# A two-layer hybrid block on one core: squares of the delta rule's rows taken four heads at a time

## The chip, the cores and the metric

The kernel runs on one core of a Trainium2 chip. The metric is device time in microseconds of one execution. The kernel before took 1170.36 us (median of three runs, 1169.89 to 1171.27).

Engines are named as in the profile: PE multiplies matrices and transposes through the identity (PEld loads its weights), DVE and ACT are the vector and the scalar engine, POOL the general one, SP issues DMAs. Each engine works through its own queue in the order in which the program was built, and an instruction at the head of a queue that waits for a semaphore holds up everything behind it.

## What is computed

256 positions of width 1024 go through two layers of `ffn`, `mixer`, `ffn`, `ple` and a last RMS norm. The mixer adds an attention over key blocks (NSA) and a gated delta rule with 4 heads of 128. Of the delta rule this matters:

```
gq, gk, gv = silu(conv(qkv)) split in three
gq, gk = x * rsqrt(sum(x * x) + 1e-6) per head
o = gated_delta_rule(gq, gk, gv, log_decay, beta)     # q is scaled by 128 ** -0.5
o = rmsnorm(o, gdn_norm) * silu(zg)
out = concatenate([o_nsa, o]) @ w_out
```

## The kernel before

Rows of x stand in two tiles of 128 positions. Every dense product is taken as three products of 128x128 by 128x512, of a high and a low part of both factors (`mm3`). Weights come by DMA in units of 128x2048, each cut into two halves; ACT writes the high part (`hi`, L158) and DVE the low part (`lo`, L159). There are five buffers each for `hi` and `lo`, so ACT can only write a high part when PE has done the last product with the one five before it.

A mixer runs seven generators side by side (`weave`, L452): the dense products of w_in (`dense`), the delta rule (`keys`, `queries`, `values`), the gates, the attention, and the output product (`project`). A `yield` hands over to another one. `weave` follows PE's planned time alone, so the order of emission has no costs of ACT, DVE or POOL in it. The framework then schedules the emitted instructions again, engine by engine, by costs of its own and by the readiness of operands and buffers; the queues that result are what runs.

The steps that the change touches, per layer:

- `squares` (L737) gives the sums of squares of the four heads of k (from `gdn_keys`, L753) and of q (from `gdn_queries`, L877), for both tiles of 128 positions. Source is a PSUM bank of 128x4x128: four ACT instructions with an accumulator each, and a `junk` output.
- From q's sums POOL makes `rqs` (L878 to L880): the norm of q, with the scale 128 ** -0.5.
- `gdn_outputs` (L925) computes the delta rule's rows `o` without q's norm; ACT copies them out of PSUM (L935).
- `gdn_finish` (L938) squares `o * rqs` per head (L947, ACT), POOL takes the power (L948, L949), DVE multiplies the two norms (L950) and then rows, norm and gate (L953); PE transposes the result (L957), ACT and DVE split it in `g` (L961, L962), on which the second half of the output product waits.

The output product (`pairs`, L342, called at L552) has 96 wide products per layer: 48 on the attention's result (`n`), then 48 on the delta rule's (`g`). They are the last work of PE in a mixer.

The attention's softmax takes, for the second tile of positions, four score banks per pair of heads: DVE adds the mask and takes the maximum (L1063), ACT does the exponential (L1070) and the scaling (L1079), PE transposes, ACT copies (L1091, `pT`), PE multiplies by the values. The output gate `zg` is the last of the dense chunks: ACT copies it (L486) and does its tanh (L695), DVE finishes it (L696). Two buffers under the tag `m2` serve the tanh, the gated rows and, in the changed kernel, the squares.

Of the kernel before, what the change touches and what calls it, by code (L numbers as in the profile page):

```python
# [12 lines left out]
BF = mybir.dt.bfloat16  # L13
AF = mybir.ActivationFunctionType
OP = mybir.AluOpType
AX = mybir.AxisListType
# [9 lines left out]
EPS = 1e-6  # L26
# [143 lines left out]
class Kern:  # L170
# [565 lines left out]

    def squares(self, ss, src):  # L737

        for h in range(4):
            junk = self.tile("junk", [128, 128], BF)  # L740
            self.nc.scalar.activation(junk, src[:, h], AF.Square, accum_out=ss[:, h:h + 1])

    def gdn_keys(self, g):

# [180 lines left out]
    def gdn_outputs(self, g):  # L925

        nc = self.nc
        g["o"] = o = self.tile("g", [128, NT, 4, 128], name="o")
        for t in range(NT):
            b = self.bank("G", [128, 4, 128])  # L930
            for h in range(4):
                if t:
                    self.mm(b[:, h], g["qe"][:, h], g["st"][:, h], True, False)
                self.mm(b[:, h], g["attn"][:, t, h], g["vn"][t][:, h], not t, True)
            nc.scalar.activation(o[:, t], b, AF.Copy)  # L935
            yield 0.4

    def gdn_finish(self, g, szg):  # L938
        nc, l, os = self.nc, self.l, g["o"]
        oh, ol, get = self.parts("g", 4)  # L940
        for t in range(NT):
            o = os[:, t]
            ss, f = self.tiny(4, "oss"), self.tiny(4, "of")
            rqs = g["rqs"][:, t]
            for h in range(4):
                junk = self.tile("junk", [128, 128], BF)
                nc.scalar.activation(junk, o[:, h], AF.Square, scale=rqs[:, h:h + 1], accum_out=ss[:, h:h + 1])  # L947
            nc.gpsimd.tensor_scalar(f, ss, 1.0 / 128, EPS, op0=OP.mult, op1=OP.add)  # L948
            nc.gpsimd.tensor_tensor(f, f, self.mhalf[:, :4], op=OP.pow)  # L949
            nc.vector.scalar_tensor_tensor(f, f, 0.5, rqs, op0=OP.mult, op1=OP.mult)  # L950
            og = self.tile("m2", [128, 4, 128])
            for h in range(4):
                nc.vector.scalar_tensor_tensor(og[:, h], o[:, h], f[:, h:h + 1], szg[:, t, h * 128:(h + 1) * 128],  # L953
                                               op0=OP.mult, op1=OP.mult)
            b = self.bank("G", [128, 4, 128])
            for h in range(4):
                self.tr(b[:, h], og[:, h])  # L957
            yield 0.5
            gn = self.sm[:, l, S_GN:S_GN + 1]
            ts = slice(t * 128, (t + 1) * 128)  # L960
            nc.scalar.activation(oh[0][:, :, ts], b, AF.Copy, scale=gn)  # L961
            nc.vector.scalar_tensor_tensor(ol[0][:, :, ts], b, gn, oh[0][:, :, ts].bitcast(F32),  # L962
                                           op0=OP.mult, op1=OP.subtract)
        g["gdn"] = get
# [177 lines left out]
```

## Time and profile before

| what | us |
|---|---|
| median of three runs | 1170.36 |
| the profiled execution | 1169.91 |
| its span, first to last instruction | 1168.1 |
| PE busy | 1143.6 |
| DVE busy | 727.9 |
| ACT busy | 666.1 |
| POOL busy | 66.5 |

The execution's own time is 1.8 us above its span. Of the span, the first mixer takes about 202 to 367 us and the second about 778 to 942 us, read from the chain of waits; the rest are feed-forward parts and `ple`. "Busy" of PE is modelled to a product's end, so that overlapping products count once and a sparse PE can still read as nearly busy.

### The profile page before, as it was taken

The page shows a single profiled execution, that of the slowest core. Times are in us where ns is not written, and L with a number is a line of the kernel's source. Part 1 is how long each engine was busy: PE and PEld are TensorE (multiplying, and loading weights), DVE is VectorE, ACT ScalarE, POOL GpSimd, SP SyncE. Part 2 cuts the span into 40 slices and gives each one's busy share as a digit, 9 for nine tenths or more (in the row PEclk, how much of TensorE's full clock was granted, in tenths as well). Part 3 has the DMA queues.
Part 4 walks back from the last instruction along what each step waited for, and adds up shares of the span by engine and source line. Part 5 has one row for each costly group of instructions (what it writes and reads, how often), then busy time and mean ns, then how long its engine had stood idle before and what let it go on. Part 6 is the DMA issues. An engine that isn't in the chain of part 4 may idle for free.

```text
span 1168.1 us, 16007 instructions
## 1 busy us (share of the span) xinstructions
PE 1143.6 (98%) x6182; PEld 924.5 (79%) x6182; DVE 727.9 (62%) x1233; ACT 666.1 (57%) x1217; POOL 66.5 (6%) x94
## 2 busy tenths in 40 slices
PE   8999999999999999999999999999999999999996
PEld 6888888878767888888878888887787678888885
DVE  5656545897756565645675555469978466555454
ACT  7545445746886454544665454366479665545363
POOL 0000000030020000000000000002300100000011
PEclk9999999999999999999999999999999999999998
DMA  8545754531114545554454565544322245455640
GB/s 325 186 176 202 259 187 137 198 139 74 70 47 147 208 172 188 188 212 150 180 204 157 216 226 207 193 155 162 109 73 100 75 151 206 156 215 190 202 176 36
DMA packets 29291, 194.27 MB, mean 166 GB/s; under 512 B 3232, under 2 KB 3616, under 8 KB 7200
## 3 DMA queue, kind: packets, MB, share of 16 engines
q1 hardware_dynamic: 28496, 191.69, 45.2%
q10 hardware_dynamic: 720, 1.57, 0.4%
q8 instruction: 48, 0.79, 0.3%
q14 instruction: 27, 0.22, 0.1%
HBM read 192.20 MB, written 1.05 MB: 165 GB/s over the span
## 4 chain that ended last, share of the span: by engine, by line
PE 90%; DVE 5%; ACT 3%; issue 1%; POOL 1%; DMA 0%; POOLq 0%; SPq 0%; ACTq 0%
PE bA L267 51%; PE bN L267 31%; PE bG L271 4%; PE bG L267 3%; DVE lo L159 1%; PE bN L271 1%; ACT hi L158 1%; ACT p L1079 1%; DVE mn L628 0%; DVE mn L618 0%; DMA x<-x 0%; DVE mn L622 0%; ACT junk L947 0%; POOL rqs L879 0%; DVE ad L786 0%
## 5 line engine op out<-in xcount | busy, mean ns | idle before, releaser
L267 PE MATMUL bA<-hi,xT 128*128 128x512 f32 (+1 forms) x1856 | 600.6, 396 | 0.9 <-DVE xT L321 0.5
L159 DVE TENSOR_TENSOR lo<-raw,hi 128x1024 fp32r<-128x1024 f32 (+2 forms) x358 | 430.6, 1207 | 214.8 <-ACT hi L158 193.7
L158 ACT ACTIVATE hi<-raw 128x1024 fp32r<-128x1024 f32 (+2 forms) x358 | 373.1, 1047 | 225.6 <-PE bN L267 122.7
L267 PEld LDWEIGHTS bA<-hi,xT 128*128 128x128 f32 x1856 | 344.2, 188 | 70.0 <-ACT xT L320 1.9
L267 PE MATMUL bA<-lo,xT 128*128 128x512 f32 (+1 forms) x928 | 360.5, 390 | 0.0
L267 PEld LDWEIGHTS bA<-lo,xT 128*128 128x128 f32 x928 | 174.9, 188 | 34.3 <-issue 1.2
L267 PE MATMUL bN<-hi,n 128*128 128x512 f32 x448 | 144.9, 396 | 1.9 <-ACT n L1101 1.9
L267 PE MATMUL bN<-hi,g 128*128 128x512 f32 x448 | 139.9, 391 | 0.0
L267 PEld LDWEIGHTS bN<-hi,n 128*128 128x128 f32 x448 | 84.3, 189 | 21.2 <-ACT n L1101 2.8
L267 PEld LDWEIGHTS bN<-hi,g 128*128 128x128 f32 x448 | 83.8, 188 | 17.2
L383 DVE SCALAR_TENSOR_TENSOR m<-bA,r,m 128x256 f32<-128x256 f32 x88 | 42.2, 479 | 79.5 <-ACT m L381 79.5
L267 PE MATMUL bN<-lo,n 128*128 128x512 f32 x224 | 89.6, 400 | 0.0
L267 PE MATMUL bN<-lo,g 128*128 128x512 f32 x224 | 87.8, 392 | 0.0
L381 ACT ACTIVATE m<-bA,r 128x256 f32<-128x256 f32 x88 | 41.4, 470 | 72.7 <-PE bA L267 69.6
L292 POOL TENSOR_SCALAR r<-ss 128x1 f32<-128x1 f32 x18 | 6.0, 331 | 839.4 <-ACT junk L285 839.4
L267 PEld LDWEIGHTS bN<-lo,n 128*128 128x128 f32 x224 | 42.6, 190 | 8.0 <-issue 0.2
L267 PEld LDWEIGHTS bN<-lo,g 128*128 128x128 f32 x224 | 42.1, 188 | 8.4
L321 DVE SCALAR_TENSOR_TENSOR xT<-bG,first,xT 128x128 fp32r<-128x128 f32 x96 | 31.6, 346 | 24.8 <-ACT xT L320 24.7
L389 ACT ACTIVATE g<-bG 128x256 fp32r<-128x256 f32 x48 | 18.0, 374 | 42.4 <-PE bG L271 42.3
L320 ACT ACTIVATE xT<-bG,first 128x128 fp32r<-128x128 f32 x96 | 32.7, 361 | 16.0 <-DVE xT L321 15.8
L271 PE MATMUL bG<-first,m 128*128 128x128 f32 x192 | 38.4, 277 | 2.0 <-DVE m L953 1.8
L271 PEld LDWEIGHTS bG<-first,m 128*128 128x128 f32 x192 | 26.3, 141 | 16.7 <-DVE m L953 3.1
(229 smaller groups left out, 957.4 us busy)
## 6 DMA issues: line engine op xcount, KB each, us to landing
raw<-up SPq DMA_DIRECT2D x86, 1024.0 KB, 4.8
raw<-dn SPq DMA_DIRECT2D x44, 1024.0 KB, 4.8
raw<-win SPq DMA_DIRECT2D x24, 1024.0 KB, 4.8
raw<-wout SPq DMA_DIRECT2D x8, 1024.0 KB, 4.9
raw<-gate SPq DMA_DIRECT2D x8, 1024.0 KB, 4.7
cw<-cw SPq DMA_DIRECT2D x8, 512.0 KB, 7.7
raw<-up SPq DMA_DIRECT2D x4, 512.0 KB, 6.7
raw<-proj SPq DMA_DIRECT2D x2, 1024.0 KB, 4.8
```

Of the source, the lines that this page charges most:

```text
L158: nc.scalar.activation(hi[:, s:f], raw[:, a + s:a + f], AF.Copy)
L159: nc.vector.tensor_tensor(lo[:, s:f], raw[:, a + s:a + f], hi[:, s:f].bitcast(F32), op=OP.subtract)
L267: self.nc.tensor.matmul(out, lhsT, rhs, start=start, stop=stop, skip_group_check=part)
L271: self.nc.tensor.transpose(out, x, self.ident[:n, :n])
L292: nc.gpsimd.tensor_scalar(r, self.ss[:, 0:1], self.ss[:, 1:2], EPS, op0=OP.add, op1=OP.add)
L320: nc.scalar.activation(hi[h][:, i, cs], b[:, i, :], AF.Copy, scale=g)
L321: nc.vector.scalar_tensor_tensor(lo[h][:, i, cs], b[:, i, :], g, hi[h][:, i, cs].bitcast(F32), op0=OP.mult, op1=OP.subtract)
L381: nc.scalar.activation(s, bs[t][:, :256], AF.Silu, scale=r[t])
L383: nc.vector.scalar_tensor_tensor(h, bs[t][:, 256:], r[t], s, op0=OP.mult, op1=OP.mult)
L389: nc.scalar.activation(hh[c // 2][o], b, AF.Copy)
L1079: nc.scalar.activation(p[kv][:, i, br], p[kv][:, i, br], AF.Copy, scale=m[:, i, br:br + 1])
```

## The change

k's and q's squares become one ACT instruction over 128x512 into an `m2` tile in 32 bits, and one DVE sum over the last axis. The rows `o` leave PSUM on DVE, times `rqs`, in place of ACT's copy. Their squares go the same new way, `rqs` is no longer a scale of the square, and the factor 0.5 and the second multiplication by `rqs` (L950) go into the constants of L948: f = (4 sum / 128 + 4 eps) ** -0.5.

```diff
     def squares(self, ss, src):
-        for h in range(4):
-            junk = self.tile("junk", [128, 128], BF)
-            self.nc.scalar.activation(junk, src[:, h], AF.Square, accum_out=ss[:, h:h + 1])
+        sq = self.tile("m2", [128, 4, 128])
+        self.nc.scalar.activation(sq, src, AF.Square)
+        self.nc.vector.tensor_reduce(ss, sq, axis=AX.X, op=OP.add)
...
-            nc.scalar.activation(o[:, t], b, AF.Copy)
+            nc.vector.tensor_tensor(o[:, t], b, g["rqs"][:, t, :, None].to_broadcast([128, 4, 128]), op=OP.mult)
...
-            rqs = g["rqs"][:, t]
-            for h in range(4):
-                junk = self.tile("junk", [128, 128], BF)
-                nc.scalar.activation(junk, o[:, h], AF.Square, scale=rqs[:, h:h + 1], accum_out=ss[:, h:h + 1])
-            nc.gpsimd.tensor_scalar(f, ss, 1.0 / 128, EPS, op0=OP.mult, op1=OP.add)
+            self.squares(ss, o)
+            nc.gpsimd.tensor_scalar(f, ss, 4.0 / 128, 4 * EPS, op0=OP.mult, op1=OP.add)
             nc.gpsimd.tensor_tensor(f, f, self.mhalf[:, :4], op=OP.pow)
-            nc.vector.scalar_tensor_tensor(f, f, 0.5, rqs, op0=OP.mult, op1=OP.mult)
```

The scheduler answers with another order in most of the mixer, on PE, DVE and ACT; in both layers the last third is ordered alike. Lines above L741 keep their numbers; behind the change they are up to four lower (L1070 becomes L1066, L1079 L1075, L1091 L1087, L1063 L1059, L953 L949).

ACT in the first mixer, around the copy of the gate's second tile (`zg`, L486). Before (`p` are the attention's probabilities, `q` the sums of q's squares):

```order
L1079 ACTIVATE p<-p,smx 128x256 x3
L158 ACTIVATE hi<-raw 128x1024
L1079 ACTIVATE p<-p,smx 128x256 x5
L1091 ACTIVATE pT<-bN 128x512
L741 ACTIVATE junk,q_3108<-bG 128x128
L1091 ACTIVATE pT<-bN 128x512
L741 ACTIVATE junk,q_3108<-bG 128x128
L1091 ACTIVATE pT<-bN 128x512
L741 ACTIVATE junk,q_3108<-bG 128x128
L695 ACTIVATE m_3186<-zg 128x512
L741 ACTIVATE junk,q_3108<-bG 128x128
L486 ACTIVATE zg<-bA,r_1621 128x512
```

The exponentials (L1070) are already done here, the scalings stand ahead of the gate's copy. In the changed kernel, from the high part of a weight half ahead of the gate:

```order
L158 ACTIVATE hi<-raw 128x1024
L695 ACTIVATE m_2951<-y 128x512
L158 ACTIVATE hi<-raw 128x1024
L695 ACTIVATE m_2974<-y 128x512
L486 ACTIVATE zg<-bA,r_1621 128x512
L1066 ACTIVATE p,smx<-p,mx 128x256 x8
L1075 ACTIVATE p<-p,smx 128x256 x8
L1087 ACTIVATE pT<-bN 128x512 x3
L740 ACTIVATE m_3119<-bG 128x512
L740 ACTIVATE m_3130<-bG 128x512
L695 ACTIVATE m_3166<-zg 128x512
L695 ACTIVATE m_3170<-zg 128x512
```

All eight exponentials and all eight scalings of the last softmax now stand behind the gate's second copy, which itself is behind two high parts.

DVE at the same place, before (`ISA p,mx` is the masked maximum of the scores, L1063):

```order
L714 SCALAR_TENSOR_TENSOR y<-bG,small,y 128x254
L1063 ISA p,mx<-bN,cst 128x256
L1063 ISA mx 128x1
L714 SCALAR_TENSOR_TENSOR y<-bG,small,y 128x253
L1067 TENSOR_SCALAR mx<-mx 128x2
L159 TENSOR_TENSOR lo<-raw,hi 128x1024
L696 SCALAR_TENSOR_TENSOR y<-m_2984,y 128x512
L1075 RECIPROCAL smx<-smx 128x4
L1076 TENSOR_TENSOR smx<-smx,sg 128x4
L1075 RECIPROCAL smx<-smx 128x4
L1076 TENSOR_TENSOR smx<-smx,sg 128x4
```

In the changed kernel:

```order
L714 SCALAR_TENSOR_TENSOR y<-bG,small,y 128x255 x2
L714 SCALAR_TENSOR_TENSOR y<-bG,small,y 128x254 x2
L714 SCALAR_TENSOR_TENSOR y<-bG,small,y 128x253 x2
L159 TENSOR_TENSOR lo<-raw,hi 128x1024
L696 SCALAR_TENSOR_TENSOR y<-m_2951,y 128x512
L159 TENSOR_TENSOR lo<-raw,hi 128x1024
L696 SCALAR_TENSOR_TENSOR y<-m_2974,y 128x512
L1059 ISA p,mx<-bN,cst 128x256
L1059 ISA mx 128x1
L1059 ISA p,mx<-bN,cst 128x256
L1059 ISA mx 128x1
L1063 TENSOR_SCALAR mx<-mx 128x2
```

Seven of the eight masked maxima have moved behind two low parts (L159) and the silu of q (L696).

PE at the end of the first mixer, before; `bG<-first,m_3236` are the transposes of the delta rule's first finished rows, `bN<-hi,n` and `bN<-lo,n` products of the output on the attention's result:

```order
L267 MATMUL bN<-pT,kv 64x256 x4
L267 MATMUL bN<-hi,n 128x512
L267 MATMUL bN<-lo,n 128x512
L267 MATMUL bN<-hi,n 128x512 x2
L267 MATMUL bN<-lo,n 128x512
L267 MATMUL bN<-hi,n 128x512 x2
L267 MATMUL bN<-lo,n 128x512
L267 MATMUL bN<-hi,n 128x512 x2
L271 MATMUL bG<-first,m_3236 128x128 x2
L267 MATMUL bN<-lo,n 128x512
L271 MATMUL bG<-first,m_3236 128x128
```

In the changed kernel, where the same rows are `m_3210` and those of the second tile `m_3233`:

```order
L267 MATMUL bN<-pT,kv 64x256 x4
L271 MATMUL bN<-first,p 128x128 x8
L271 MATMUL bG<-first,m_3210 128x128 x4
L267 MATMUL bN<-pT,kv 64x256 x4
L271 MATMUL bG<-first,m_3233 128x128
L267 MATMUL bN<-hi,n 128x512
L271 MATMUL bG<-first,m_3233 128x128
L267 MATMUL bN<-lo,n 128x512
L267 MATMUL bN<-hi,n 128x512 x2
L267 MATMUL bN<-lo,n 128x512
```

The transposes now stand ahead of all 48 of these products; before, ten of them in this piece and six further up stood in front.

## Rows read from the trace of the kernel before

**Rows 1.** the page's first rows: span; busy us, share of the span, instructions
```profile
span 1168.1 us, 16007 instructions
...
PE 1143.6 (98%) x6182; PEld 924.5 (79%) x6182; DVE 727.9 (62%) x1233; ACT 666.1 (57%) x1217; POOL 66.5 (6%) x94
```

**Rows 2.** stretches (us): busy us and instructions (x) by engine, granted clock, DMA
```profile
245.00:260.00 15.00, 13.52 (x125) 10.30 (x125) 14.96 (x22) 7.19 (x9) 3.90 (x3) 1.00 0.42 146
320.00:335.00 15.00, 14.57 (x97) 10.12 (x96) 9.90 (x25) 14.98 (x41) 1.30 (x1) 1.00 0.29 112
335.00:350.00 15.00, 13.16 (x65) 9.53 (x64) 5.81 (x14) 9.71 (x31) 4.76 (x7) 0.89 0.05 9
911.00:926.00 15.00, 13.12 (x73) 9.46 (x72) 6.16 (x15) 10.23 (x31) 4.76 (x7) 1.00 0.06 9
```

**Rows 3.** what PE waited for in the first mixer: total us, times, longest
```profile
PE bN L267 <- ACT n L1101: 0.9, 1, 0.9
PE bG L271 <- DVE m L953: 0.9, 1, 0.9
PE bN L271 <- DVE mn L626: 0.9, 1, 0.9
PE bG L267 <- DVE T L833: 0.7, 2, 0.5
```

**Rows 4.** PE in order of time: start us, length us
```profile
305.22 1.05 PE L267 MATMUL bG<-vb,W 128*128 128x128 f32 x8
...
354.53 0.39 PE L267 MATMUL bN<-hi,g 128*128 128x512 f32 x1
...
881.56 1.05 PE L267 MATMUL bG<-vb,W 128*128 128x128 f32 x8
...
929.62 0.39 PE L267 MATMUL bN<-hi,g 128*128 128x512 f32 x1
```

**Rows 5.** the chain of waits, a dense stretch of PE: start, us, what, products
```profile
139.08 49.43 PE bN L267 x218
```

**Rows 6.** ACT groups of 290 to 350 us: count, busy us, mean ns, idle
```profile
L158 ACT ACTIVATE hi<-raw 128x1024 fp32r<-128x1024 f32 x8 | 8.4, 1054 | 3.8 <-PE bN L267 2.9 <-PE bA L267 0.9
L1070 ACT ACTIVATE p<-p,mx 128x256 f32<-128x256 f32 x16 | 8.0, 500 | 0.0
L1079 ACT ACTIVATE p<-p,smx 128x256 f32<-128x256 f32 x16 | 6.7, 499 | 0.0
L1091 ACT ACTIVATE pT<-bN 128x512 f32<-128x512 f32 x11 | 6.5, 589 | 0.0
...
L695 ACT ACTIVATE m<-y 128x512 f32<-128x512 f32 x4 | 2.5, 619 | 0.0
L741 ACT ACTIVATE junk<-bG 128x128 bf16<-128x128 f32 x8 | 2.3, 284 | 0.0
...
L947 ACT ACTIVATE junk<-o,rqs 128x128 bf16<-128x128 f32 x8 | 3.2, 399 | 2.1 <-POOL rqs L880 2.0
```

**Rows 7.** DVE groups, 290 to 350 us, same columns
```profile
L159 DVE TENSOR_TENSOR lo<-raw,hi 128x1024 fp32r<-128x1024 f32 x7 | 8.6, 1224 | 1.4 <-ACT hi L158 1.4
...
L696 DVE SCALAR_TENSOR_TENSOR y<-m,y 128x512 f32<-128x512 f32 x4 | 2.8, 688 | 0.7 <-ACT m L695 0.7
...
L1023 DVE TENSOR_REDUCE m<-pc 128x8 f32<-128x128 f32 x1 | 0.3, 275 | 0.0
```

**Rows 8.** the norms' chain in order of time, all engines
```profile
337.35 0.25 POOL L878 TENSOR_SCALAR q<-q 128x8 f32<-128x8 f32 x1 [9.97 <-ACT junk L741]
...
339.73 0.40 ACT L947 ACTIVATE junk<-o,rqs 128x128 bf16<-128x128 f32 x1 [1.98 <-POOL rqs L880]
...
342.56 0.19 POOL L948 TENSOR_SCALAR of<-oss 128x4 f32<-128x4 f32 x1 [2.87 <-ACT junk L947]
...
343.90 0.16 DVE L950 SCALAR_TENSOR_TENSOR of<-of,rqs 128x4 f32<-128x4 f32 x1 [1.08 <-POOL of L949]
...
344.10 1.14 DVE L953 SCALAR_TENSOR_TENSOR m<-o,of,zg 128x128 f32<-128x128 f32 x4
```

## The prediction

> **What bounds the kernel now.** I read the page first: PE is busy in 98% of a span of 1168.1 us [rows 1], so a change pays only where PE waits or runs thin. The chain of waits gives the price of a dense stretch: 218 wide products in 49.43 us, 0.227 each [rows 5]. In the first mixer the waits of PE itself are few [rows 3]: 0.9 us each for the last attention rows (n L1101) and the first gated rows (m L953) at the end, and 0.9 and 0.7 for DVE's rope and triangular inverse near its middle. The table by stretch [rows 2] shows why. From 320 to 335 us ACT is busy in 14.98 of 15 us, and yet PE loses only 0.43 of 15: its queue has dense products between the steps of the attention. From 335 to 350 PE has 65 products in 15 us, and the granted clock is 0.89; the second mixer's same stretch has 73 and a clock of 1.00. From 245 to 260 DVE is the full engine, 14.96 of 15. So three places decide: what DVE gets in the front of the mixer, who waits for ACT in its last third, and how much dense work stands beside the delta rule's last chain.
>
> I measure the last third between two marks: PE's first product with W on `vb`, and its first output product on the delta rule's rows `g`. Before, that is 354.53 - 305.22 = 49.31 us in the first mixer and 929.62 - 881.56 = 48.06 in the second [rows 4]. The orders are the same, and the first shows the lower clock [rows 2]: I book the difference of 1.25 as the price of one drop. Both programs have issued the same products of PE when they reach the first mark, and the same between the marks, so only waits and clock can differ.
>
> **What is removed and added.** Per layer ACT loses 16 small squares for k and q, of 0.28 us and an accumulator read behind each, 8 of 0.40 for o [rows 6], and the two copies of o; it gets six squares of 128x512. The trace has none; I take 0.59, as for a copy out of PSUM of that size (L1091: 6.5/11 [rows 6]). DVE gets six sums of 128x512 and the two products that write o. The trace has a sum of 128x128 at 0.275 [rows 7]; from below a sum cannot be cheaper than that, from above it is a 128x1024 operation, 1.22 (L159). I take 0.6, near the 0.69 of a two-input 128x512 operation (L696), less some overlap. L950 goes.
>
> **Front of the mixer: 0, from -1.6 to +1.5 per layer.** The two sums for k put 1.2 us on DVE before its full stretch. Ahead of that stretch DVE still waits for weights' high parts, so part of it is hidden, and ACT is done with k's squares over 1 us sooner (8 x 0.28 and their reads, against 1.2). In the new order PE takes twelve wide products, 2.7 us, more ahead of the first inverse product, which covers the rope's wait of 0.9, and has as much less between the inverse's levels, where 0.7 is waited now [rows 3]. These nearly cancel. If all 1.6 went, it were -1.6; if the sums stood on the path whole, +1.2, and I put that end at +1.5 for what queues behind them.
>
> **Last third, by the new queues, in the clock of the first mixer's rows.** Start both at 305.22.
>
> 1. In the new order PE runs all the gate's products (40 wide ones from the mark on, 9.1 us) with six of the eight score products (1.4) and the small products between them (6.1, by the first mark's eight records in 1.05 [rows 4]) without interruption. They end at 321.9; before, some of the gate's products were kept for between the exponentials. ACT's high part for the next weight half needs the buffer of the gate's last half, so it cannot start before 322.2: 1.05 to the end, then a tanh 0.62 and the gate's copy 0.6, 324.3.
> 2. DVE's low part follows that high part, then the silu of q that needs the tanh: about 325.1. Only now come the seven masked maxima. The first exponential has its maxima at 326.0. Meanwhile PE waits for the silu of q (1.6 and 0.8 us).
> 3. ACT has eight exponentials at 0.50 (8.0/16) and eight scalings at 0.42 (6.7/16) [rows 6] in one piece, 7.4 us: 333.4. The first `pT` copy, 0.5, comes behind: 333.9. PE has two score products, q's products with k and two rounds of transposes as DVE and ACT free their banks, and is through with them at about 329.6; its next product needs this `pT`. It stands still for 4.2 us. Before, PE had transposes and dense products between the exponentials here.
> 4. Two more `pT`, two squares, two tanh, three `pT`: 1.1 + 1.2 + 1.25 + 1.6 = 5.2, so ACT is through at 339.1. Beside it q's sums on DVE end near 336.9, POOL takes 2.4 (337.35 to 339.73 [rows 8]): `rqs` at 339.3. PE has o's first tile at 339.4 and the second at 341.1.
> 5. o on DVE 0.65, square 0.55, sum 0.6, POOL 1.35 (342.56 to 343.90 [rows 8]): 342.7. Four gated rows 1.14 (344.10 [rows 8]): 343.8. The second tile's sum stands behind these on DVE: 344.4, POOL 1.35, first gated row 0.35: 346.1. This chain is about as long as before, where the first gated rows start at 344.10: the added wait (o for `rqs`) is paid by the squares saved.
> 6. Only then does PE get to the attention's half of the output product, since the second tile's first transpose stands ahead of it: 48 products at 0.227 and four transposes, 11.4 us, so `g` starts at 357.5. Before, sixteen of the 48 were spent during the chain.
>
> That is 52.3 us between the marks against 49.31 and 48.06: +3.0 and +4.2, sum +7.2.
>
> **Clock.** The starved piece, 322 to 346 us, is longer than the one that cost 1.25 before, with one stop of 4 us. I book one such drop in each mixer: +2.5. At least 0; at most, with half clock through o's products (2.7 us, on the path, of which 1.5 shows) and the first 2 us of the dense block, 3.5 each.
>
> The Trainium skill (TensorE: Matmul & The Clock Gate, "What's actually happening") says that the throttled clock is the default and that activity lifts it. The trace bears that out only in part: of two stretches with the same waits, one shows 0.89 and one 1.00. By the rule alone the lower clock would hold through the starved piece in both mixers, which is the first rival below.
>
> **Sum.** Against the execution's own 1169.91 (the median of the runs is 1170.36, 0.45 above): 1169.91 + 7.2 + 2.5 = 1179.6. I call it 1179.5. What a measurement can tell from no change is 0.2%, 2.3 us.
>
> **Rivals.**
>
> - *The clock stays low through the whole starved piece of both mixers.* For it: the 0.89 came with waits of one us only. Against it: PE does get some products there. 1169.91 + 7.2 + 7 = 1184. Chance 0.2.
> - *The front pays it back.* If the waits of 1.6 in the front go in both layers, the sums cost 0.275 (three stand in the last chain, 1 us less per layer), and the clock holds, then 1169.91 + 7.2 - 3.2 - 2 = 1171.9, no change. For it: the new order has more dense work there. Against it: DVE is the full engine and gets more. Chance 0.08.
> - *ACT's load is what counts, faster.* ACT is full from 320 to 335 [rows 2], and loses at least 8 x 0.28 + 8 x 0.40 + 2 x 0.59 - 4 x 0.59 = 4.3 us per layer in the last third, the reads not counted. If the softmax is through early for that, PE's waits at the end, 0.9 + 0.9 [rows 3], and the 0.43 that it loses from 320 to 335 go, with the drop of 1.25: 1169.91 - 2 x 2.2 - 1.25 = 1164.2. It decides if the first exponential starts before 323 us; that asks for the high part not to wait for the gate's last product, against the five buffers. Chance 0.07.
>
> The likeliest case, ordinary clock, has the remaining 0.65 and runs from 1174 to 1184 by the bounds of the front (3 each way) and one drop more or less. The range for 8 in 10 is 1172 to 1187: it takes in the low clock with a late front and leaves out the faster case and part of the no-change one. Faster 0.06, same 0.09, slower 0.85.
>
> **What would show it.** In the changed profile PE should wait about 4 us for a `pT` copy (L1087) near 330 us and 906 us, and 1 to 1.6 for the silu of q (L696); the first of the eight exponentials should start about 326; `rqs` should be ready near 339 and the first gated row (L949) near 343; 48 wide products on `n` should follow the second tile's first transposes without a break; the two marks should lie 52 us apart, more with a granted clock below 0.95 there. ACT's busy sum should fall by some 16 to 20 us and DVE's rise by 9. The prediction is wrong if the marks are under 50 us apart, if exponentials run before the gate's second copy, or if the loss stands in the front (before 305 us) instead.

## The result, and the profile after

The changed kernel takes 1182.63 us (median of five runs, 1179.98 to 1184.06), the kernel before 1171.16 in runs on the same chip: a ratio of 1.0099, 95% interval 1.0085 to 1.0113. It is slower by 11.5 us. The profiled execution is the slowest of the five, 1184.06 us with a span of 1182.1, 14.15 above the profiled execution before, so the rows below add up to somewhat more than the medians do.

The page's first rows, after (before: [rows 1]):

```profile
span 1182.1 us, 15943 instructions
...
PE 1146.4 (97%) x6182; PEld 929.2 (79%) x6182; DVE 736.9 (62%) x1245; ACT 655.3 (55%) x1129; POOL 75.1 (6%) x94
```

DVE has gained the 9 us that were forecast. ACT has lost 10.8, not 16 to 20: the accumulator reads behind the small squares of [rows 6] last 9.7 us in all, but overlap their neighbours so far that they made up only 2.6 of ACT's busy time, which counts an overlap once.

The table by stretch, after: us, then busy us and instructions (x) of PE, PEld, DVE, ACT and POOL, the granted clock, and the DMA columns. The first two stretches are of the first mixer, the others of the second (before: [rows 2]).

```profile
320.00:335.00 15.00, 9.04 (x49) 7.67 (x48) 10.49 (x33) 11.81 (x32) 1.28 (x1) 0.89 0.21 70
335.00:350.00 15.00, 13.85 (x80) 9.17 (x80) 6.46 (x13) 8.46 (x16) 4.86 (x7) 0.77 0.01 2
...
905.00:920.00 15.00, 8.30 (x49) 5.74 (x50) 9.58 (x30) 12.20 (x34) 1.28 (x1) 0.90 0.20 70
920.00:935.00 15.00, 13.64 (x84) 9.18 (x83) 7.67 (x17) 6.68 (x12) 4.86 (x7) 0.88 0.00 1
```

From 320 to 335 us PE falls from 14.57 busy us to 9.04 and from 97 products to 49. The granted clock is below 1.00 in all four stretches; before, it was in one of the three of [rows 2] that lie in the last thirds. It knows two levels here, and a value between them is a mean: it stood at half, 1.2 GHz, in these three pieces (0.51 by their rounded edges), two of the first mixer's last third and one of the second's, and at full clock between them.

```profile
326.30:329.80 3.50, 3.50 (x17) 3.31 (x16) 3.50 (x18) 2.51 (x11) 0.93 (x1) 0.51 0.37 154
336.60:343.50 6.90, 6.64 (x30) 4.59 (x29) 2.83 (x5) 3.23 (x6) 2.43 (x3) 0.51 0.00 0
916.80:923.70 6.90, 6.17 (x25) 2.86 (x26) 2.61 (x4) 4.31 (x9) 2.43 (x3) 0.51 0.01 2
```

The PE waits of the whole run, after: us in total, times, longest (before: [rows 3], the first mixer's):

```profile
PE bN L267 <- ACT pT L1087: 8.0, 3, 4.0
...
PE bG L267 <- DVE y L696: 4.5, 4, 1.7
PE bG L271 <- DVE m L949: 2.4, 3, 1.0
```

PE in order of time, after: start, us, operation, [idle before it and what ended that]. The prediction's two marks are the `vb,W` products and the first on `g` (before: [rows 4]).

```profile
305.47 0.38 PE L267 MATMUL bG<-vb,W 128*128 128x128 f32 x2
...
322.08 0.39 PE L267 MATMUL bA<-hi,xT 128*128 128x512 f32 x1
324.21 1.13 PE L267 MATMUL bG<-y 128*128 128x128 f32 x8 [1.75 <-DVE y L696]
...
330.26 0.93 PE L271 MATMUL bG<-first,y 128*128 128x128 f32 x7
...
335.06 1.14 PE L267 MATMUL bN<-pT,kv 128*64 128x256 f32 x8 [3.76 <-ACT pT L1087]
...
341.14 1.91 PE L267 MATMUL bG<-y,attn 128*128 128x128 f32 x8
...
350.27 0.33 PE L271 MATMUL bG<-first,m 128*128 128x128 f32 x1 [1.02 <-DVE m L949]
350.36 0.48 PE L267 MATMUL bN<-hi,n 128*128 128x512 f32 x1
...
361.70 0.39 PE L267 MATMUL bN<-hi,g 128*128 128x512 f32 x1
...
887.91 0.27 PE L267 MATMUL bG<-vb,W 128*128 128x128 f32 x1
...
917.53 0.70 PE L267 MATMUL bN<-pT,kv 128*64 128x256 f32 x2 [3.97 <-ACT pT L1087]
...
943.88 0.39 PE L267 MATMUL bN<-hi,g 128*128 128x512 f32 x1
```

The marks are 361.70 - 305.47 = 56.23 us apart in the first mixer and 943.88 - 887.91 = 55.97 in the second, against 49.31 and 48.06 before: +6.92 and +7.91, together 14.8. The whole difference of the two profiled executions, 14.15, stands between the marks; the rest of the program is 0.7 shorter.

All engines in the first mixer, after, same columns; it answers to [rows 8]:

```profile
325.95 1.28 POOL L795 TENSOR_TENSOR qe<-y,eg 128x512 f32<-128x512 f32 x1 [50.15 <-DVE y L696]
...
326.41 0.84 DVE L1063 TENSOR_SCALAR mx<-mx 128x2 f32<-128x2 f32 x1
...
327.29 0.51 ACT L1066 ACTIVATE p<-p,mx 128x256 f32<-128x256 f32 x1 [2.52 <-DVE mx L1063]
...
343.16 0.69 DVE L935 TENSOR_TENSOR o<-bG,rqs 128x512 f32<-128x512 f32 x1 [3.97 <-PE bG L267]
343.94 0.63 ACT L740 ACTIVATE m<-o 128x512 f32<-128x512 f32 x1 [1.97 <-DVE o L935]
344.61 0.69 DVE L741 TENSOR_REDUCE oss<-m 128x4 f32<-128x512 f32 x1 [0.76 <-ACT m L740]
...
346.72 1.14 DVE L949 SCALAR_TENSOR_TENSOR m<-o,of,zg 128x128 f32<-128x128 f32 x4 [0.83 <-POOL of L946]
347.78 0.68 DVE L741 TENSOR_REDUCE oss<-m 128x4 f32<-128x512 f32 x1
...
349.87 0.62 DVE L949 SCALAR_TENSOR_TENSOR m<-o,of,zg 128x128 f32<-128x128 f32 x2 [1.41 <-POOL of L946]
```

The product that writes o waits for PE (3.97), not for q's norm, which was ready 2.7 us earlier. The first exponential waits for a negated maximum of 128x2 elements that takes 0.84 us here and 0.16 elsewhere; POOL's `qe` ends just with it.

### The profile page after: what moved, and what is told of

Same layout as the page of the kernel before. It is cut to its first block, busy times and chain, and to the rows that moved or that the text cites. A ratio compares the mean times of both kernels' runs of the same rounds, so it can differ in the third digit from the quotient of the medians.

```text
span 1182.1 us, 15943 instructions
## 1 busy us (share of the span) xinstructions
PE 1146.4 (97%) x6182; PEld 929.2 (79%) x6182; DVE 736.9 (62%) x1245; ACT 655.3 (55%) x1129; POOL 75.1 (6%) x94
## 3 DMA queue, kind: packets, MB, share of 16 engines
HBM read 192.20 MB, written 1.05 MB: 163 GB/s over the span
## 4 chain that ended last, share of the span: by engine, by line
PE 90%; DVE 4%; ACT 3%; POOL 1%; issue 1%; DMA 0%; POOLq 0%; SPq 0%; ACTq 0%; DVEq 0%
PE bA L267 50%; PE bN L267 31%; PE bG L271 4%; PE bG L267 4%; PE bN L271 1%; ACT hi L158 1%; ACT p L1066 1%; DVE lo L159 1%; ACT p L1075 1%; DMA x<-x 0%; POOL ab L816 0%; POOL of L946 0%; POOL kn L889 0%; DVE m L949 0%; DVE oss L741 0%
## 5 line engine op out<-in xcount | busy, mean ns | idle before, releaser
L159 DVE TENSOR_TENSOR lo<-raw,hi 128x1024 fp32r<-128x1024 f32 (+2 forms) x358 | 431.9, 1211 | 224.4 <-ACT hi L158 202.9
L267 PE MATMUL bN<-hi,n 128*128 128x512 f32 x448 | 141.8, 390 | 0.0
```

The costliest lines, as they stand in the source:

```text
L159: nc.vector.tensor_tensor(lo[:, s:f], raw[:, a + s:a + f], hi[:, s:f].bitcast(F32), op=OP.subtract)
L267: self.nc.tensor.matmul(out, lhsT, rhs, start=start, stop=stop, skip_group_check=part)
```

## The experiments

Two theories stood against each other. *Order*: the loss comes from the queues that the scheduler made, whatever the new operations cost. *Cost*: it comes from the six sums and two products that DVE got, and from the waits that they bring. Ten kernels ran, all timed against the kernel before (1170.4 to 1170.7 us in those sets).

**k's squares alone.** The kernel before with the wide square and the sum for `k2` only; q's and o's stay as they were.

```diff
-            self.squares(k2[:, t], b)
+            self.squares1(k2[:, t], b)    # wide square into m2, one sum on DVE
```

> Only k's squares are taken four heads at a time; q's and o's squares, ACT's copy of o and the second norm stay as in the kernel before. With that alone the queues of the mixer's middle are already those of the changed kernel: eight exponentials and eight scalings behind the gate's second copy. Order theory (the loss comes from these queues, whatever the new operations cost): most of the loss is here, 1178 to 1183 us, the marks of the first mixer at least 54 us apart, PE waiting about 4 us for the first pT copy. Cost theory (the loss is the six sums and two products that DVE got and o's wait for q's norm): two of six sums and none of the waits are left, at most 2 us above the kernel before, 1171 to 1174, marks 49 to 51 apart.

It took 1184.32 us, ratio 1.0118 (1.0104 to 1.0131), with the marks 56.53 and 57.47 us apart: the whole loss, and a little more (1.3 us above order's range). The waits of PE and the first mixer's stretches:

```profile
PE bN L267 <- ACT pT L1097: 9.8, 6, 2.4
```

```profile
320.00:335.00 15.00, 9.73 (x57) 7.72 (x55) 10.53 (x32) 13.39 (x35) 1.28 (x1) 0.89 0.20 70
335.00:350.00 15.00, 12.31 (x79) 8.32 (x76) 1.39 (x6) 9.86 (x39) 3.39 (x5) 0.89 0.00 1
```

The hole from 320 to 335 is there without one changed operation in the last third. Two pairs of instructions per layer, some 90 us ahead of the hole, are enough to turn the queues. (The longest wait for pT is 2.4 where 4 was expected: it falls into more pieces.)

**The rest of the change.** The changed kernel with k's squares head by head again, in a function `squares4` with the old text.

```diff
-            self.squares(k2[:, t], b)
+            self.squares4(k2[:, t], b)
```

> The changed kernel with k's squares taken head by head again; q's and o's squares and the product that takes o out of PSUM are new. The queues then mix exponentials, scalings and the gate's products as in the kernel before. Order theory: 1167 to 1172 us, marks of the first mixer 47 to 50 us apart, clock 1.00 or close to it from 320 to 335 us. Cost theory: four of six sums and all of the waits on q's norm are kept, so most of the loss is, 1178 to 1182, marks above 53.

1169.87 us, ratio 0.9997 (0.9989 to 1.0006); marks 47.81 and 49.16. The stretches of its first mixer:

```profile
320.00:335.00 15.00, 14.57 (x102) 11.19 (x101) 10.84 (x27) 14.59 (x33) 2.67 (x3) 1.00 0.34 126
335.00:350.00 15.00, 12.68 (x68) 8.94 (x68) 10.04 (x19) 6.67 (x10) 3.22 (x6) 1.00 0.01 2
```

Four of the six sums, both products on o and the chain over q's norm are in, and with the ACT work that they save they cost nothing that can be measured. That chain is not idle: o's product waits for `rqs` here (DVE stands still for 2.47 us before it), as in five of the orders of the changed kernel below, but PE has other work meanwhile. Cost has fallen for these parts.

**All of it, in another order.** Every operation of the change, with k's squares written to another buffer.

```diff
-        sq = self.tile("m2", [128, 4, 128])
+        sq = self.tile("ab", [128, 4, 128])    # for k alone
```

> The changed kernel, every operation of it, with one edit: k's squares go to the buffer under the tag ab in place of m2. The scheduler then orders the middle of the mixer in a third way, with the gate's second copy behind all exponentials and scalings. Order theory: 1166 to 1173 us, since dense products stand between the exponentials again; marks 47 to 51 us apart. Cost theory: no operation is gone, so 1180 to 1184.

1170.62 us, ratio 1.0004 (0.9995 to 1.0013); marks 49.87 and 51.20, with five dense products (1.1 us) more between them than before. The name of one buffer is worth 12 us. Nor do k's squares hold an `m2` buffer that the hole waits for: in the changed kernel their sums have read them by 231.4 us, some 90 us ahead of it. What the name changes is the order.

**Another lag, and a miss.**

```diff
-    LAG = 1.4
+    LAG = 1.2
```

> The changed kernel with the constant that stretches the lags of the emission at 1.2 in place of 1.4: the same operations, and queues in which the gate's products stand late, between the output's products on n and the first gated rows, so that PE has 49 wide products in front of the first transposes of gated rows. Order theory: the last chain is covered by dense work, 1163 to 1172 us, granted clock 1.00 through the last third. Cost theory: 1180 to 1184.

1182.92 us, ratio 1.0113 (1.0097 to 1.0128): order's number was missed by ten. All engines at the end of its first mixer, in order of time:

```profile
341.64 1.29 DVE L935 TENSOR_TENSOR o<-bG,rqs 128x512 f32<-128x512 f32 x2 [2.24 <-POOL rqs L880]
...
349.96 0.67 ACT L486 ACTIVATE zg<-bA,r 128x512 f32<-128x512 f32 x1
350.66 0.63 ACT L695 ACTIVATE m<-zg 128x512 f32<-128x512 f32 x1
351.20 0.61 ACT L740 ACTIVATE m<-o 128x512 f32<-128x512 f32 x1
352.02 0.68 DVE L741 TENSOR_REDUCE oss<-m 128x4 f32<-128x512 f32 x1
...
354.62 1.17 PE L271 MATMUL bG<-first,m 128*128 128x128 f32 x4 [6.15 <-DVE m L949]
```

I had counted the 49 products as cover for the last chain. But the gate is part of that chain, its products are now the last of the 49, and on ACT the squares of o stand behind the gate's copy and tanh: o is out of PSUM at 342.9, its square starts at 351.20, and PE stands for 6.15 us with nothing left to do. The clock did not hold either: 0.66 from 350 to 365 us. It is an order that can be read as a bad one before it runs. For cost the number is right, but the chain is late by 8.3 us of queue, not by 0.68 us of sum.

**Step 6 alone.** One more yield in `gdn_finish`; the queues of all engines but PE are unchanged, and on PE 12 of the 48 products on `n` stand ahead of the second tile's transposes.

```diff
+            if t:
+                yield 3.0
             b = self.bank("G", [128, 4, 128])
```

> The changed kernel with the second tile's transposes of gated rows emitted 3 us later. The queues of ACT, DVE, POOL and SP stay word for word; on PE, 12 of the 48 products on n stand ahead of these four transposes in place of one. If step 6 of the prediction is a cost of its own (PE held for the second tile's rows, about 1.4 us idle and 1.4 us of interleaving per layer in the changed profile), 1177 to 1180.5 us. If the end of the mixer is set elsewhere, by the rows g themselves, it stays at 1182 to 1184.

1180.11 us, ratio 1.0080 (1.0067 to 1.0092), 2.5 us under the changed kernel by the medians, though the two intervals overlap; the marks come 1.74 and 2.10 us closer. Not all of that is step 6. DVE and PE at the end of the first mixer:

```profile
345.94 1.14 DVE L949 SCALAR_TENSOR_TENSOR m<-o,of,zg 128x128 f32<-128x128 f32 x4 [0.83 <-POOL of L946]
...
359.93 0.39 PE L267 MATMUL bN<-hi,g 128*128 128x512 f32 x1
```

From the first gated row to the first product on `g`, the piece that the edit touches, are 13.99 us here and 14.98 (346.72 to 361.70) in the changed kernel; in the second mixer 13.97 and 15.01. So step 6 is a cost of its own of 1.0 us per layer, the smaller part of the loss. The other 0.8 and 1.1 lie ahead of it, where the queues are word for word the same and the half clock fell at other times (333.3 to 340.3 us in the first mixer).

**The softmax in one piece.** One lag of q's convolution.

```diff
-            yield from until(z, "gq", 1.0)
+            yield from until(z, "gq", 3.0)
             yield from self.conv(g, "q", z["gq"], 0)
```

> The changed kernel, all its operations and buffers, with one constant: the convolution of q is emitted 3.0 in place of 1.0 lag units after its rows. The queues are the same up to the last third, and there the first exponentials stand ahead of the gate's second copy again, with gate products between the scores. Theory of the softmax in one piece: the 4 us wait for pT goes in both layers, and with it the low clock, 1168 to 1173 us. Rival, that the loss sits in the later chain (o, sums, norm, 48 products): 1178 to 1183.

1173.62 us, ratio 1.0027 (1.0018 to 1.0036): 9.0 of the 11.5 us come back, 0.6 us short of the range expected. PE's wait for `pT` is 1.2 us in all instead of 8.0, and the marks are 51.81 and 51.36 apart. It still waits 3.8 us for q's silu and 4.8 for gated rows, and the low clock is not all gone: 0.89 from 335 to 350 us.

**The clock.** Products that nobody reads, in a stream of their own that the scheduler may place.

```diff
+            yield from until(z, "zg", 0.0)
+            for _ in range(7):
+                b = self.bank("A", [128, 512])
+                for _ in range(4):
+                    nc.tensor.matmul(b, hx[:, 0, :128], hx[:, :2].rearrange(...), start=True, stop=True)
+                yield 0.5
```

> The changed kernel with 28 extra wide products per mixer whose result nobody reads, placed by the scheduler where PE stands still behind the gate's products and ahead of the first pT product: 28 x 0.227 = 6.4 us of work more per mixer, against some 6 us of waits there; 12 of them overfill the wait for q's silu by 0.8 us. The output is unchanged. Clock theory (2 to 3 us per layer of the loss are half clock behind the stop, from 335 to 343 us): the granted clock from 320 to 350 us is 1.00 or near it, and the time falls, 1176 to 1181. Theory of waits alone: the work adds its overfill, 1183 to 1187, whatever the clock shows.

1178.17 us, ratio 1.0063 (1.0050 to 1.0075): 12.7 us of products more, and 4.5 us less time. Its first mixer, the stretches, then PE and the first DVE product on o in order of time (L510 are the added products):

```profile
320.00:335.00 15.00, 13.96 (x78) 11.30 (x76) 10.68 (x33) 11.81 (x31) 1.28 (x1) 1.00 0.21 70
335.00:350.00 15.00, 13.46 (x93) 9.29 (x94) 8.80 (x18) 8.95 (x17) 4.61 (x7) 1.00 0.01 2
```

```profile
322.50 2.34 PE L510 MATMUL bA<-xT 128*128 128x512 f32 x8
...
331.25 2.77 PE L510 MATMUL bA<-xT 128*128 128x512 f32 x11
335.26 0.65 PE L267 MATMUL bN<-pT,kv 128*64 128x256 f32 x4 [1.24 <-ACT pT L1097]
...
339.40 1.06 PE L267 MATMUL bG<-y,attn 128*128 128x128 f32 x8
...
340.57 0.69 DVE L945 TENSOR_TENSOR o<-bG,rqs 128x512 f32<-128x512 f32 x1 [0.29 <-PE bG L267]
```

The first `pT` comes no earlier (335.26 against 335.06), but from there to o's products PE needs 4.14 us instead of 6.08, and eight of these take 1.06 instead of 1.91. The marks are 53.23 and 53.28 us apart, 3.00 and 2.69 less than in the changed kernel, and in the first mixer 2.8 of the 3.00 lie between the first `pT` and o on DVE (5.31 us against 8.10). Most of it was half clock behind the stop. Not strictly all: with the added products the scheduler also put two `pT` copies per layer ahead of a tanh of the gate, with PE's order to match; in the changed kernel PE had waited 0.26 us there.

**An order that beats both.** The changed kernel with a shorter lag behind the scores.

```diff
-                yield 1.6
+                yield 0.8
```

> The changed kernel with the lag behind a softmax's score products at 0.8 in place of 1.6. The queues mix the gate's products with scores, transposes and values through the whole last third, and about 30 of the 48 products on n stand ahead of the second tile's transposes. Order theory: no wait over 1 us and no low clock in the last third, 1163 to 1170 us. Cost theory: not under 1178.

1161.48 us, ratio 0.9921 (0.9907 to 0.9934). Its first mixer:

```profile
320.00:335.00 15.00, 15.00 (x106) 11.49 (x107) 8.05 (x21) 11.58 (x26) 3.47 (x4) 1.00 0.19 71
335.00:350.00 15.00, 13.85 (x68) 10.68 (x65) 11.62 (x21) 8.47 (x11) 3.33 (x4) 1.00 0.40 140
```

It is faster than order's range by 1.5 us. PE has no gap from 320 to 335 and the clock is 1.00 throughout; one wait over 1 us is left in each last third, 1.15 for gated rows. The marks are 47.24 and 47.25 apart, with three dense and eight small products more between them. Of the 8.9 us that its span (1159.2) lies under that of before, 2.9 are between the marks and 5.8 ahead of them: 2.5 ahead of the first, 3.3 from the first mixer's end to the second. As those eleven products per layer have moved behind the first mark, this is no split by cause; what helps where I did not take apart. Two more runs ask how far the lag itself does it. With 1.0 in place of 0.8:

> The changed kernel with the same lag at 1.0. The middle of the last third is ordered nearly as with 0.8; at its end 19 products on n are left behind the second tile's transposes, where 0.8 leaves 9, and the gate's second copy comes later against the softmax. Order theory: each product left behind costs at most 0.227 us, 10 of them 2.3 per layer if the wait ahead is as long, so 1161 to 1168 us. Cost theory: not under 1178.

1165.77 us, ratio 0.9959 (0.9946 to 0.9971), marks 49.55 and 49.62: 2.3 per layer more, the number that the ten products more behind the transposes gave. The granted clock is 0.89 from 335 to 350 us here and 1.00 with 0.8, so the ten products need not be all of it. And with 0.8 in the kernel before:

> The kernel before, none of the change in it, with the lag behind a softmax's score products at 0.8 in place of 1.6 as in the run at 1161.48 us. Its queues also mix the gate's products with scores and values, and 38 of the 48 products on n stand ahead of the second tile's last transposes. If the gain of that run belongs to the order alone, 1161 to 1166 us; if it needs the change's wide squares (ACT with 88 instructions less), 1168 to 1172.

1179.96 us, ratio 1.0076 (1.0062 to 1.0090). Neither expectation holds. The end of its first mixer, all engines:

```profile
349.08 0.40 ACT L947 ACTIVATE junk<-o,rqs 128x128 bf16<-128x128 f32 x1
...
350.01 0.59 PE L271 MATMUL bG<-first,m 128*128 128x128 f32 x2 [2.48 <-DVE m L953]
...
352.41 0.39 ACT L947 ACTIVATE junk<-o,rqs 128x128 bf16<-128x128 f32 x1
...
356.09 0.50 PE L271 MATMUL bG<-first,m 128*128 128x128 f32 x2 [0.47 <-DVE m L953]
```

The last of eight small squares of o stands on ACT behind a high part of a weight and the first tile's `g`, so it starts 3.3 us after the seventh. With one wide square a tile no such split can happen. But it isn't the loss: PE stands for only 0.47 us before the second tile's transposes, and in the second mixer no wait shows before them. PE's longest waits are 2.48 and 2.46 us for the first tile's gated rows, and in the second mixer the clock fell besides (half from 914.9 to 921.8 and from 932.0 to 935.5 us; marks 52.62 and 56.08 apart). So a lag that makes the changed kernel 21 us faster makes the kernel before 10 us slower, and how much of the 18 us between the two is due to the wide squares stays open.

## Why the prediction held, point by point

The time lies 3 us above the forecast and inside the range, and the loss is where it was said to be. By its steps, first mixer:

1. *Gate's last product 321.9, high part 322.2, gate's copy done 324.3.* The last product started at 322.08 and ended at 322.47, the high part started at 322.64, the copy was done at 324.76; the high part stood behind another one and a tanh. (The forecast's own terms, 1.05, 0.62 and 0.6 from 322.2 on, add up to 324.5, not 324.3.)
2. *Silu of q 325.1, first exponential 326.0.* The silu ended 0.7 later, and the exponential started at 327.29, since the negated maximum took 0.84 us beside POOL. PE waited 1.75 and 0.52 for the silu where 1.6 and 0.8 were said.
3. *Eight exponentials and scalings 7.4 us, PE stands still for 4.2.* 327.29 to 334.43 is 7.1; PE stood for 3.76 in the first mixer and 3.97 in the second. The experiment on q's lag shows that this order, with the stop and what follows from it, is most of the loss.
4. *ACT through at 339.1, rqs 339.3, o's first tile 339.4.* This is the step that was mis-sized. From the first `pT` product to o on DVE were 5.5 us by the prediction (333.9 to 339.4), and are 8.1 (335.06 to 343.16). PE ran at half clock (1.2 GHz) from 336.6 to 343.5, and ACT waited for its transposes (1.62 us at 340.5), not the other way round. With the added products, at full clock, the same piece took 5.31: the step was sized for a clock that PE did not have.
5. *Chain as long as before.* From o on DVE to the first gated rows 3.56 us (343.16 to 346.72) against 3.3; a sum takes 0.68 where 0.6 was taken. (The forecast's terms from 339.4 on add up to 342.55, not 342.7.) That the chain over q's norm costs no time in the whole is shown by the run with k's squares undone.
6. *48 products and four transposes, 11.4 us.* From 350.27 to 361.70, 11.43.

The products on `g` started at 361.70 where 357.5 was said. Of these 4.2 us 0.25 are the later first mark, 0.9 came up to the first `pT`, 2.6 in step 4 and 0.4 behind it.

**The clock** was the wrong term: 2.5 us booked for both mixers. The added products gave 3.0 + 2.7 = 5.7 back between the marks. With that in place of 2.5, the prediction's own sum is 1169.91 + 7.2 + 5.7 = 1182.8. The median of 1182.63 is near that partly by luck: the sum starts from the profiled execution before, and the profiled one after is 1184.06, 1.3 above it. So the first rival, given 0.2, had the mechanism right: the clock is low behind the stop in both mixers. It had the clock low through the whole starved piece, and a price of 3.5 each; measured, it was at half for 6.9 us behind the stop in each mixer, and for 3.5 more in the first ahead of it, where PE waited for ACT anyway, and the dense block ran at full clock from its first product. The prediction weighed it down because one of two equal mixers had kept its clock before; there, the waits were of 0.9 us. The rule cited from the Trainium skill (TensorE: Matmul & The Clock Gate, "What's actually happening"), that activity lifts the clock, agrees with the trace: below 1.00 in all four starved stretches, 1.00 with the added products, which are activity and nothing else. Why the fall comes when it does no run here shows: in the first mixer 1.5 us after the stop had ended (335.06), in the second 0.7 us before its end (917.53).

**The front** was put at 0: the first mark is 0.25 later, and the piece from the first mixer's end to the second mark 0.8 shorter. The sums for k on DVE cost nothing that shows there. The rival in which the front pays back had the right sign with a fifth of its size (0.6 in all, against 3.2); the faster one asked for an exponential before 323 us and got it at 327.3.

What the prediction didn't ask is why the queues moved at all. It took them from the built program, which was right, and so had no need to know; but the change's fate hung on k's two squares, which it costed at nothing, rightly, and on the buffer that they were given.

## What to carry to other kernels

Where a scheduler orders the queues, read the built order at the places with least slack before pricing the new instructions: here the same operations gave 1161 to 1183 us by their order. Look there for a run of one engine's work behind a wait of another's (eight exponentials behind a gate's copy), for what the last dense block stands behind, and whether each operand of the chain that it should cover is ready ahead of it. Price a stop of PE with what comes behind it at half clock, and try several harmless draws of the order before judging an edit.

## What the runs showed of the hardware

- 56 more products, 12.7 us of work, made the kernel 4.5 us faster, with the granted clock at 1.00 in both mixers' last thirds instead of 0.77 to 0.90.
- The queues of both mixers are alike, and the clock can differ: in the run with k's squares undone 1.00 from 335 to 350 us and 0.89 in the second mixer's like stretch (909.8 to 924.8), in the kernel before with the short lag 1.00 and 0.77 (914 to 929), with marks 52.62 and 56.08 apart.
- DVE's negated maximum over 128x2 takes 0.16 us, and 0.84 while POOL multiplies `q` by `eg` (325.95 to 327.23); it ends at 327.25, with POOL. The Trainium skill (SBUF — State Buffer, "Who interferes with whom") says that operations of this kind can take the pair of ports that DVE and POOL share, and that whichever of the two issues first then holds it for its whole instruction while the other is blocked. The two ends, 0.02 us apart, agree.
